# Chunk inverses folded into the operands that read the state, and attention blocks kept within their logits' PSUM banks

## The chip, the core and the metric

The kernel runs on one core of one Trainium2 chip. The metric is the device time of one execution in microseconds, the median over several runs. The engines named below are TensorE (PE, with its weight loads as PEld), VectorE (DVE), ScalarE (ACT), GpSimd (POOL) and SyncE (SP). The PSUM memory that receives matmul results is used here in banks of 128x512 words of 32 bits.

## The reference

One residual block over 512 tokens of 1024 channels, in 32-bit floats:

```
x = x + 0.5 * swiglu(rms_norm(x), w1, w3, w2)            # FFN 1
p = rms_norm(x) @ w_in                                   # r,k,v,codes | q,k,v,f | gates A,B
y_a = rwkv7_mixer(token_shift(p_rwkv)) @ rwkv_proj       # 8 heads x 64
y_b = forgetting_attention(p_fox) @ fox_proj             # 8 heads x 64
x = x + (sigmoid(gA) * y_a + sigmoid(gB) * y_b) @ w_out
x = x + 0.5 * swiglu(rms_norm(x), ...)                   # FFN 2
out = rms_norm(x)

def step(state, inp):                                    # inside rwkv7_mixer, over the 512 tokens
    sa = einsum('bhvk,bhk->bhv', state, a_t)
    state = state * w_t + sa (x) b_t + v_t (x) k_t
    y_t = einsum('bhvk,bhk->bhv', state, r_t)
```

The attention is causal softmax attention whose logits carry a bias, the sum of log forget gates between key and query; q and k are normalized per head.

## The kernel before

**Tiling.** Activations are held transposed, channels on the 128 partitions, 512 tokens in the free dimension. A product of a 1024-row input with 128 columns of a weight matrix is eight `mm3` groups. `mm3` (L122) is three matmuls of 128x128 on 128x512: the weights and the activations are each split in a rounded high part and a remainder, and high x high (L123), high x low (L124) and low x high (L125) are summed. The weights come from DRAM (SP's queue) as `raw`, ACT rounds them to `whi` (L115), DVE subtracts to `wlo` (L116). FFN 1 comes first, then the mixers, the projection `w_out`, FFN 2 and the final norm.

**The recurrence.** The 512 tokens are cut into NC = 16 chunks of C = 32. The eight heads are four pairs p with two halves q. `step(p)` (L507) makes for each pair the operand `G[p][q]` with an a-part (index 0) and an r-part (index 1), and `BK`; products `gp` of BK with G (L569), masked, fill the other 64 rows of G. For the a-part this is the strictly lower triangular matrix L of the chunk, 32x32; it goes to DRAM (`Ld`) and its rows in G are set to zero. After all four steps DVE computes the inverses (I - L)^-1 of all 128 triangles at once (`TT`, L612 and L614, last instruction `inv`), and these go through DRAM (`Td`) into `Tall`, 64-row blocks with two heads each on their diagonal. The loop over chunks (L718) then is, with R the state and the chunk's rows of v and u stacked:

- `xps` = G's a-part on R: eight matmuls (L725), then DVE copies it to `Xs` (L728): first hop
- `ups` = inverse on Xs: four matmuls (L732), then ACT copies it in four pieces into R (L734, L735): second hop
- `sps` = `Dt` on R, the next state: eight matmuls (L739), then two DVE multiplications by the decay PC write it into the next R (L741): third hop
- `yps` = the output, from G's r-part on R (L748), copied by ACT into V4

Every second chunk `stage(c)` (L701) transposes v and BK for two chunks ahead (`vp`, `bp`), and ACT copies them (L713, L714).

**What stands between the hops.** The loop is unrolled, and the scheduler orders the instructions of the whole kernel by its own simulation. Two devices steer it: `tc.issue_after(x)` puts what is inside behind instruction x, and the list `holes` holds matmuls of the chain (two entries each for xps, ups and sps of every chunk) behind which, one after another, the `mm3` groups of columns made by `cols(..., holes)` are put. This filler are the columns of q and k (`load_qk(p)`, L644, bank `pq`) and of gates (`gate`, bank `pgt`, of which `early(m)`, L638, stores the second half's). `plain_gate` (L496) makes a gate's column without holes: eight of these, one inside each step and four ahead of the chunk loop, and eight `early` ones.

**Attention** runs for pairs of heads p = 0..3 beside the chain. For each pair the operands `qa`, `kb`, `klc`, `qb` are made (L786 to L792) on DVE and ACT. Then come three blocks of queries, (0, 1), (2) and (3), each for both halves q: logits `lp` in a bank of `pf` (L804 to L806), maximum on DVE (L812), exponential on ACT (L813), scaling on DVE (L818), transposes (`tpp`, L824) into another bank of `pf`, ACT copy `tr` (L826), the product with v (`av`, L835) in the bank of the second tpp, DVE copy (L837). Pool `pf` has three banks, `pr` (for xps, ups, sps, yps, vp and bp) three, `pm` (for pq and pgt) two. After the loop come the group norm of the recurrence's output (`yc`, `pg`), the two projections and w_out.

Of the kernel before, what the change touches and what calls it, by code (L numbers as in the profile page):

```python
# [9 lines left out]
F32 = mybir.dt.float32  # L10
# [8 lines left out]
P = 128  # L19
T = 512  # L20
# [30 lines left out]
def kernel(  # L51
# [330 lines left out]
    with ExitStack() as mx:  # L382
# [4 lines left out]
        G = [[sp.tile([P, NC, 2, C], F32, name=f"G{p}{q}", tag=f"G{p}{q}") for q in range(2)] for p in range(NP)]  # L387
# [59 lines left out]
        zslots = [h for g in G[3] for h in (g[:, 0:8], g[:, 8:16])] + [BKs[3][:, 0:8], BKs[3][:, 8:16]]  # L447
        zslots = [h.rearrange("p c a t -> p (c a t)") for h in zslots] + spare[0:2]
# [58 lines left out]
        def step(p):  # L507
# [41 lines left out]
            for q in range(2):  # L549
                s = slice(q * 64, (q + 1) * 64)  # L550
                dve.scalar_tensor_tensor(G[p][q][s, :, 0, :], ch(kk)[s], -1.0, Pp[s, :, 0:C],
                                         op0=ALU.mult, op1=ALU.mult)
            for q in range(2):
                s = slice(q * 64, (q + 1) * 64)
                dve.tensor_tensor(G[p][q][s, :, 1, :], ch(r)[s], Pp[s, :, 1:C + 1], op=ALU.mult)
# [4 lines left out]
            gps = [pr.tile([P, 8, 2, C], F32, tag="b", name="gp") for _ in range(2)]  # L560
            for a_ in range(2):
                with tc.issue_after(mms[5].ins):
                    for c in range(8):
                        for q in range(2):
# [4 lines left out]
                            gm = pe.matmul(gps[g][o, c], BK[s, cc], G[p][q][s, cc], start=True, stop=True)  # L569
                for q in range(2):  # L570
# [3 lines left out]
                        G[p][q][o, g * 8:(g + 1) * 8].rearrange("p c a t -> p c (a t)"),  # L574
                        gps[g][o].rearrange("p c a t -> p c (a t)"),
                        gmask[o].rearrange("p a t -> p (a t)").unsqueeze(1).broadcast_to([64, 8, 2 * C]),
                        op=ALU.mult)
            for q in range(2):
                r0 = (1 - q) * 64
                un = (q * NP + p) * NC  # L580
                nc.gpsimd.dma_start(Ld[un:un + NC].rearrange("c s t -> s c t"), G[p][q][r0:r0 + C, :, 0, :])
                pool.memset(G[p][q][r0:r0 + C, :, 0, :], 0.0)
# [33 lines left out]
        Tb = Tall[:].rearrange("p (a c t) -> p a c t", a=2, c=NC)  # L616
        tv = Td[:].rearrange("(q i u) s t -> q i s u t", q=2, i=2)
        for i in range(2):
            for q in range(2):
                o = i * 64 + q * C  # L620
                (nc.scalar, nc.gpsimd)[q].dma_start(
                    Tb[o:o + C].rearrange("p a c t -> p (a c) t")[:, :, q * C:(q + 1) * C], tv[q, i])
# [15 lines left out]
        def early(m):  # L638
            g = xp.tile([P, T], F32, tag="acc", name="gs", bufs=2)
            gate(COL_GB, m, g[:])  # L640
            nc.sync.dma_start(gsave[KD + m], g[:])
# [364 lines left out]
```

## Time and profile before

| | |
|---|---|
| median of 3 runs | 1218.38 us (1218.21 to 1218.86) |
| profiled execution, its own time | 1219.17 us |
| its span in the profile | 1217.5 us |
| mean granted TensorE clock | 0.993 |
| PE, PEld busy share | 98%, 78% |
| DVE, ACT, POOL busy share | 54%, 37%, 8% |

The span goes from the first to the last instruction of the profiled execution. All times are microseconds unless marked ns. L123 is line 123 of the kernel file, and the lines of the changed kernel after the chunk loop stand some 30 lower. In a row of a timeline stand the start, the duration, engine, line, operation, result and operands, shapes, the number of instructions joined in the row and, in brackets, the engine's idle time before it and what ended it. In a row of groups (one that begins with L) stand the busy time of all and the mean ns of one behind the bar, then the engine's idle time ahead of them. In a row of windows stand the length, then busy time and instructions of PE, PEld, DVE, ACT and POOL, the granted clock, the DMA share and the GB/s.

### The profile page before, as it was taken

What the parts mean: (1) busy time and instruction counts of PE and PEld (TensorE: products, weight loads), DVE (VectorE), ACT (ScalarE), POOL (GpSimd) and SP (SyncE); (2) the same over time, 40 slices, a digit from 0 to 9 for tenths busy, and PEclk for the clock granted to TensorE, in tenths of its full rate; (3) what the DMA queues carried; (4) which work ended last, traced back from release to release, by engine and by line L of the source; (5) the groups of instructions that cost most, each with busy time, mean ns of one, the idle gap of its engine ahead of it and who ended that gap; (6) DMA issues with size and microseconds to landing.
All of it is one profiled execution on the core that took longest, in us unless ns stands there. A gap on an engine that the chain in (4) does not pass through costs nothing. (4 is left out here: it accounts for less than half of the span.)

```text
span 1217.5 us, 15845 instructions
## 1 busy us (share of the span) xinstructions
PE 1189.2 (98%) x6340; PEld 954.3 (78%) x6340; DVE 655.5 (54%) x974; ACT 448.9 (37%) x723; POOL 102.5 (8%) x145
## 2 busy tenths in 40 slices
PE   8999999999999999999999998999999999999997
PEld 6888888888887787886766765878888888888887
DVE  6455544543334688686566656665545455442232
ACT  6222222222224754246777547232322222222221
POOL 4100000001111112401000110111000000000110
PEclk9999999999999999999999999999999999999999
DMA  6333333233333333444121250632333333323331
GB/s 185 98 90 101 92 99 104 88 94 113 113 105 100 102 109 105 125 116 110 54 59 62 95 164 26 199 104 87 104 99 91 104 94 97 100 82 95 95 96 69
DMA packets 208088, 122.54 MB, mean 101 GB/s; under 512 B 9902, under 2 KB 200430, under 8 KB 208014
## 3 DMA queue, kind: packets, MB, share of 16 engines
q1 hardware_dynamic: 201934, 108.41, 30.5%
q0 software_dynamic: 3840, 12.32, 3.2%
q10 hardware_dynamic: 2240, 0.79, 0.3%
q8 instruction: 50, 0.82, 0.3%
q14 instruction: 24, 0.20, 0.0%
HBM read 110.82 MB, written 10.68 MB: 100 GB/s over the span
## 5 line engine op out<-in xcount | busy, mean ns | idle before, releaser
L115 ACT CAST whi<-raw 128x1024 fp32r<-128x1024 f32 (+3 forms) x199 | 198.3, 998 | 627.7 <-PE pa L124 178.8
L116 DVE TENSOR_TENSOR wlo<-raw,whi 128x1024 fp32r<-128x1024 f32 (+2 forms) x198 | 229.3, 1159 | 123.7 <-ACT whi L115 121.6
L123 PE MATMUL pa<-xh,whi 128*128 128x512 f32 x344 | 134.6, 391 | 0.0
L125 PE MATMUL pb<-xh,wlo 128*128 128x512 f32 x344 | 133.9, 389 | 0.7 <-DVE wlo L116 0.7
L123 PE MATMUL pb<-xh,whi 128*128 128x512 f32 x344 | 134.2, 390 | 0.0
L125 PE MATMUL pa<-xh,wlo 128*128 128x512 f32 x344 | 133.9, 389 | 0.0
L124 PE MATMUL pa<-xl,whi 128*128 128x512 f32 x344 | 133.8, 389 | 0.0
L124 PE MATMUL pb<-xl,whi 128*128 128x512 f32 x344 | 133.8, 389 | 0.0
L125 PE MATMUL pd<-hh,wlo 128*128 128x512 f32 x330 | 131.2, 398 | 0.0
L123 PE MATMUL pd<-hh,whi 128*128 128x512 f32 x330 | 130.3, 395 | 0.0
L124 PE MATMUL pd<-hl,whi 128*128 128x512 f32 x330 | 130.3, 395 | 0.0
L333 DVE TENSOR_TENSOR fb<-pb,rstd 128x512 f32<-128x512 f32 x43 | 29.7, 691 | 137.2 <-PE pb L125 137.2
L125 PEld LDWEIGHTS pb<-xh,wlo 128*128 128x128 f32 x344 | 64.6, 188 | 14.7 <-DVE wlo L116 1.1
L123 PEld LDWEIGHTS pa<-xh,whi 128*128 128x128 f32 x344 | 64.6, 188 | 13.9 <-issue 0.5
L123 PEld LDWEIGHTS pb<-xh,whi 128*128 128x128 f32 x344 | 64.6, 188 | 13.6 <-ACT whi L115 0.2
L124 PEld LDWEIGHTS pa<-xl,whi 128*128 128x128 f32 x344 | 64.6, 188 | 13.5 <-issue 0.2
L124 PEld LDWEIGHTS pb<-xl,whi 128*128 128x128 f32 x344 | 64.6, 188 | 13.5 <-issue 0.2
L125 PEld LDWEIGHTS pa<-xh,wlo 128*128 128x128 f32 x344 | 64.5, 188 | 13.5
L124 PEld LDWEIGHTS pd<-hl,whi 128*128 128x128 f32 x330 | 62.0, 188 | 14.9
L123 PEld LDWEIGHTS pd<-hh,whi 128*128 128x128 f32 x330 | 62.0, 188 | 14.8 <-issue 0.2
L125 PEld LDWEIGHTS pd<-hh,wlo 128*128 128x128 f32 x330 | 62.0, 188 | 14.8 <-issue 0.2
L329 DVE TENSOR_TENSOR fa<-pa,rstd 128x512 f32<-128x512 f32 x43 | 29.7, 692 | 73.1 <-PE pa L125 72.9
(367 smaller groups left out, 1960.8 us busy)
## 6 DMA issues: line engine op xcount, KB each, us to landing
raw<-in_ffn_w_dram SPq DMA_DIRECT2D x118, 512.0 KB
raw<-in_w_in_dram SPq DMA_DIRECT2D x40, 512.0 KB
raw<-in_ffn_w_dram SPq DMA_DIRECT2D x15, 384.0 KB
raw<-in_w_out_dram SPq DMA_DIRECT2D x8, 512.0 KB
xin<-in_x_dram SPq DMA_DIRECT2D x4, 512.0 KB
xsave<-xT POOLq DMA_DIRECT2D x8, 256.0 KB, 2.3
gsave<-gs POOLq DMA_DIRECT2D x8, 256.0 KB, 2.6
gsave<-gs SPq DMA_DIRECT2D x8, 256.0 KB
```

Of the source, the lines that this page charges most:

```text
L115: act.copy(hi[:], raw[:])
L116: (eng or dve).tensor_tensor(lo[:], raw[:], hi[:].bitcast(F32), op=ALU.subtract)
L123: pe.matmul(ps, whi, xhi, start=first, stop=False)
L124: pe.matmul(ps, whi, xlo, start=False, stop=False)
L125: return pe.matmul(ps, wlo, xhi, start=False, stop=last)
L329: dve.tensor_tensor(a[:], pa[:], nrm.rstd[:], op=ALU.mult)
L333: dve.tensor_tensor(b[:], pb[:], nrm.rstd[:], op=ALU.mult)
```

## The change

**The inverses.** The operand that reads the state is multiplied by the inverse once, ahead of the loop, so that `ups` comes from R in one step. `G` is laid out as [2][NC][C] instead of [NC][2][C], so that the a-part of four chunks is one contiguous 128-column block. After the columns of v, PE transposes these blocks (32 transposes, `gtr`) and ACT copies them to `GT`. `Tall` is now filled as `Tn`, with the inverses of two neighbouring chunks of one head on the diagonal of a 64x64 block. 64 matmuls `wps` multiply GT by Tn, and 16 evictions, half on ACT and half on DVE, write the result over G's a-part. In the loop, xps, Xs and the old ups are gone; eight matmuls `ups` read G and R, and one ACT copy and one DVE copy put the result in R.

**Filler.** `holes` gets two entries each for ups and sps of a chunk, and five for wps. `load_qk` is split in `load_qk` (columns) and `norm_qk`. The columns of pair 1 are made ahead of the recurrence, and the gate column NP + 3 moves from there into `early`: seven plain gates and nine early ones. The decay logs and the norm of pair 1 are put behind the first chunk's state eviction (`begun`) instead of behind `inv`.

**Attention.** The transposes go into the bank of their own logits, and `av` into the second of these; a block uses two banks of pf.

```diff
-        G = [[sp.tile([P, NC, 2, C], F32, name=f"G{p}{q}", tag=f"G{p}{q}") for q in range(2)] for p in range(NP)]
+        G = [[sp.tile([P, 2, NC, C], F32, name=f"G{p}{q}", tag=f"G{p}{q}") for q in range(2)] for p in range(NP)]
...
-        Tb = Tall[:].rearrange("p (a c t) -> p a c t", a=2, c=NC)
-        tv = Td[:].rearrange("(q i u) s t -> q i s u t", q=2, i=2)
...
+        Tn = Tall[:].rearrange("p (u t) -> p u t", t=2 * C)
+        tv = Td[:].rearrange("(u g i) s t -> g i s u t", g=2, i=2)
+        for g in range(2):
+            for i in range(2):
+                o = g * 64 + i * C
+                (nc.scalar, nc.gpsimd)[i].dma_start(Tn[o:o + C, :, i * C:(i + 1) * C], tv[g, i])
...
-        def early(m):
+        def early(n):
+            m = n + NP + 3
             g = xp.tile([P, T], F32, tag="acc", name="gs", bufs=2)
-            gate(COL_GB, m, g[:])
-            nc.sync.dma_start(gsave[KD + m], g[:])
+            gate(COL_GA, m, g[:])
+            nc.sync.dma_start(gsave[m], g[:])
...
-        def load_qk(p):
+        def load_qk(p, holes=()):
             both = []
             for c0, par0 in ((COL_Q, PAR_Q), (COL_KF, PAR_K)):
...
+                mix.cols(ps[:], *load_w(win(c0 + p * P), KD, P), P, holes)
+                if p < NP // 2:
+                    act.copy(o[:], ps[:])
+                else:
+                    dve.tensor_tensor(o[:], ps[:], mix.rstd[:], op=ALU.mult)
...
+        def norm_qk(p):
+            if p < NP // 2:
+                for o, par0 in qks[p]:
+                    dve.tensor_tensor(o[:], o[:], mix.rstd[:], op=ALU.mult)
...
+        for q, p in [(q, p) for q in range(2) for p in range(NP)]:
+            ps = bank("gtr", pr)
+            for j in range(4):
+                pe.transpose(ps[:, j * P:(j + 1) * P], G[p][q][:, 0, j * 4:(j + 1) * 4, :].rearrange("p c t -> p (c t)"), ident[:])
+            GT[q, p] = t2.tile([P, T], F32, name=f"GT{p}{q}", tag=tags[q * NP + p])
+            act.copy(GT[q, p][:], ps[:])
         plain_gate(NP)
         plain_gate(NP + 1)
         load_qk(0)
-        plain_gate(NP + 2)
-        ahead = plain_gate(NP + 3)[-1]
+        load_qk(1)
+        ahead = plain_gate(NP + 2)
+        with tc.issue_after(inv.ins):
+            norm_qk(0)
...
+        for q in range(2):
+            for p0 in range(0, NP, 2):
+                wps = [pr.tile([P, 2, 4, 2 * C], F32, tag="b", name="wps") for _ in range(2)]
+                with tc.issue_after(ahead[2 * q + p0 // 2 + 4].ins):
+                    for p in (p0, p0 + 1):
+                        for j in range(4):
+                            for g in range(2):
+                                hw = pe.matmul(wps[g][:, p - p0, j, :], GT[q, p][half(g), j * P:(j + 1) * P],
+                                               Tn[half(g), (q * NP + p) * 4 + j, :], start=True, stop=True)
+                for p in (p0, p0 + 1):
+                    for g in range(2):
+                        to = G[p][q][:, 0].rearrange("p (j g i) t -> p g j (i t)", g=2, i=2)[:, g]
+                        if g:
+                            act.copy(to, wps[g][:, p - p0])
+                        else:
+                            dve.tensor_copy(to, wps[g][:, p - p0])
+                holes.append(hw)
+        holes.append(hw)
...
-            xps = pr.tile([P, 2, 64], F32, tag="b", name="xps")
+            ups = pr.tile([P, NP, 64], F32, tag="b", name="ups")
             for p, q in heads():
...
-            Xs = sp.tile([P, 2, 64], F32, tag="Xs", name="Xs", bufs=2)
-            dve.tensor_copy(Xs[:], xps[:])
-            ups = pr.tile([P, 2, 64], F32, tag="b", name="ups")
-            for p in range(NP):
-                h = half(p // 2)
-                hu = pe.matmul(ups[h, p % 2, :], Tb[h, p % 2, c, :], Xs[h, p % 2, :], start=True, stop=True)
-            for i in range(2):
-                act.copy(R[64:96, 2 * i:2 * i + 2, 0, :], ups[64 * i:64 * i + 32])
-                act.copy(R[0:32, 2 * i:2 * i + 2, 1, :], ups[64 * i + 32:64 * i + 64])
+                o = (1 - q) * 64
+                hu = pe.matmul(ups[o:o + C, p, :], G[p][q][:, 0, c, :], R[:, p, q, :], start=True, stop=True,
+                               tile_position=(0, o))
+            act.copy(R[64:96, :, 0, :], ups[64:96])
+            dve.tensor_copy(R[0:32, :, 1, :], ups[0:32])
...
-            holes += [hx, hx, hu, hu, hs, hs]
+            holes += [hu, hu, hs, hs]
+            if c == 0:
+                begun = decay
...
-        aside.enter_context(tc.issue_after(inv.ins))
+        aside.enter_context(tc.issue_after(begun.ins))
...
+        norm_qk(1)
         aside.close()
-        load_qk(1)
...
-                    tpp = pf.tile([P, T], F32, tag="b", name="tpp")
-                    tpps.append(tpp)
+                    tpp = lps[q]
...
-                av = tpps[1]
+                av = lps[1]
...
-                if p < NP // 2 and i == 0:
-                    load_qk(p + NP // 2)
-                elif p == 1 and i == 2:
-                    early(0)
-                    early(1)
-                elif p >= NP // 2:
-                    early(3 * p - 4 + i)
+                if p == 0 and i < 2:
+                    load_qk(i + 2, holes)
+                    norm_qk(i + 2)
+                elif 3 * p + i < 3 * NP - 1:
+                    early(3 * p - 2 + i)
```

The rest of the diff adapts the other readers of G to its new layout, and applies the last gate columns' tanh only where `gate` has not done it.

**What moves.** PE ahead of the loop. Before, the last columns of the gate (pgt) are followed directly by the first chunk's xps:

```order
L124 MATMUL pgt<-xl_2596,whi 128x512
L125 MATMUL pgt<-xh_2595,wlo 128x512
L123 MATMUL pgt<-xh_2689,whi 128x512
L124 MATMUL pgt<-xl_2690,whi 128x512
L125 MATMUL pgt<-xh_2689,wlo 128x512
L725 MATMUL xps<-RD_4196,G_2702 32x64
L725 MATMUL xps<-RD_4196,G_2703 32x64
```

Now the products wps stand there, in two stretches among filler, and the first ups follows the last of them (the numbers tell buffers apart; GT_3999 to GT_4020 are the four pairs of the second half q):

```order
L743 MATMUL wps<-Tall,GT_3999 128x64 x8
L743 MATMUL wps<-Tall,GT_4006 128x64 x8
L743 MATMUL wps<-Tall,GT_4013 128x64 x4
L743 MATMUL wps<-Tall,GT_4020 128x64 x4
L123 MATMUL pq<-xh_2125,whi 128x512
L124 MATMUL pq<-xl_2126,whi 128x512
L125 MATMUL pq<-xh_2125,wlo 128x512
L123 MATMUL pq<-xh_2219,whi 128x512
L124 MATMUL pq<-xl_2220,whi 128x512
L743 MATMUL wps<-Tall,GT_4013 128x64 x4
L743 MATMUL wps<-Tall,GT_4020 128x64 x4
L763 MATMUL ups<-RD_4284,G_2702 32x64
L763 MATMUL ups<-RD_4284,G_2703 32x64
```

Where columns of a gate stood ahead of the chain, wps and columns of q stand.

DVE at the same place in the changed kernel: copies of wps into G (L751), operands of the first pair of attention heads (L820 to L823), and then the first chunk's copy of ups into R (L766). The names are those of the section on the kernel:

```order
L820 TENSOR_TENSOR qa_5085<-qk_4090,qa_5085 64x512
L751 COPY G_2706<-wps 128x4x64
L751 COPY G_2708<-wps 128x4x64
L821 CAST kb_5086<-qk_4123 64x512
L822 CAST kb_5086<-qk_4123 64x512
L823 TENSOR_TENSOR klc_5045<-qk_4123,kb_5086 64x512
L821 CAST kb_5087<-qk_4123 64x512
L822 CAST kb_5087<-qk_4123 64x512
L823 TENSOR_TENSOR klc_5046<-qk_4123,kb_5087 64x512
L751 COPY G_2703<-wps 128x4x64
L751 COPY G_2705<-wps 128x4x64
L751 COPY G_2707<-wps 128x4x64
```

The evictions of the second half's wps stand behind four casts and two differences.

DVE at the change from one pair of heads to the next, before; the row of L741 is the state's eviction:

```order
L788 CAST kb_5654<-qk_5218 64x512
L789 CAST kb_5654<-qk_5218 64x512
L792 CAST qb_5114<-sel 64x512
L812 TENSOR_REDUCE mx_5367<-lp 128x1
L790 TENSOR_TENSOR klc_5013<-qk_5218,kb_5654 64x512
L788 CAST kb_5655<-qk_5218 64x512
L789 CAST kb_5655<-qk_5218 64x512
L792 CAST qb_5115<-sel 64x512
L812 TENSOR_REDUCE mx_5368<-lp 128x1
L787 TENSOR_TENSOR qa_5652<-qk_5183,qa_5652 64x512
L741 TENSOR_TENSOR RD_4196<-sps,PC 64x4x64 x2
```

And now; L772 is the state's eviction, L766 the copy of ups:

```order
L772 TENSOR_TENSOR RD_4284<-sps,PC 64x4x64 x2
L820 TENSOR_TENSOR qa_5438<-qk_4156,qa_5438 64x512
L821 CAST kb_5441<-qk_4189 64x512
L822 CAST kb_5441<-qk_4189 64x512
L825 CAST qb_5083<-sel 64x512
L845 TENSOR_REDUCE mx_5103<-lp 128x1
L848 RECIPROCAL mx_5102<-mx_5102 128x1
L820 TENSOR_TENSOR qa_5439<-qk_4156,qa_5439 64x512
L673 SCALAR_TENSOR_TENSOR qk_5307<-qk_5307,par,qrn 128x512
L823 TENSOR_TENSOR klc_5046<-qk_4189,kb_5441 64x512
L766 COPY RD_4284<-ups 32x4x64
```

The operands that stood ahead of a state's eviction now stand between one and the copy of ups.

65 lines of the change are left out of this document (27 added, 38 removed).

## The prediction

> **What bounds the kernel now.** I read the page first: is there an engine that could give time back by being relieved?
>
> ```profile
> span 1217.5 us, 15845 instructions
> PE 1189.2 (98%) x6340; PEld 954.3 (78%) x6340; DVE 655.5 (54%) x974; ACT 448.9 (37%) x723; POOL 102.5 (8%) x145
> ```
>
> TensorE (PE) is at work for 1189.2 of 1217.5 us. The change can therefore win in two ways only: by taking matmul work away, or by closing the 28 us in which PE waits, together with what a reduced clock costs. So the second view is the busy time by stretches of 20 us through the stage that the change touches (PE, PEld, DVE, ACT, POOL, then the granted clock):
>
> ```profile
> 541.00:561.00 20.00, 18.87 (x100) 14.47 (x98) 12.70 (x29) 9.55 (x18) 3.83 (x8) 1.00 0.73 185
> 561.00:581.00 20.00, 18.86 (x197) 13.85 (x196) 16.19 (x28) 15.29 (x35) 0.00 (x0) 1.00 0.10 28
> 581.00:601.00 20.00, 20.00 (x225) 15.77 (x222) 9.80 (x24) 14.47 (x41) 0.00 (x0) 1.00 0.19 54
> 661.00:681.00 20.00, 18.15 (x185) 13.46 (x181) 12.71 (x28) 12.85 (x34) 0.55 (x1) 0.91 0.20 61
> 721.00:741.00 20.00, 15.56 (x85) 9.84 (x84) 6.73 (x17) 10.76 (x22) 1.64 (x3) 0.83 0.36 120
> 741.00:761.00 20.00, 18.10 (x65) 11.77 (x65) 16.99 (x28) 16.09 (x28) 0.00 (x0) 1.00 0.09 27
> 541.00:701.00 160.00, 151.67 (x1468) 113.75 (x1467) 100.91 (x215) 108.16 (x266) 8.21 (x16) 0.99 0.28 80
> ```
>
> From 541 to 701 us, nearly the whole recurrence, PE waits for 160 - 151.67 = 8.3 us, and the clock of 0.91 in one stretch costs 0.09 x 20 = 1.8 us more. The end of attention, 721 to 761 us, waits 4.44 + 1.90 = 6.3 us and loses 0.17 x 20 = 3.4 us of clock. That is 19.8 us, all that there is to win besides work. Third, which waits these are, from PE's timeline:
>
> ```profile
> 557.30 0.49 PE L140 MATMUL pq<-shi,bonesr 128*128 128x512 f32 x1 [0.58 <-ACT shi L136]
> 558.76 0.44 PE L732 MATMUL ups<-Xs,Tall 64*64 64x64 f32 x4 [0.47 <-DMA Tall<-Td]
> 570.03 0.33 PE L739 MATMUL sps<-RD,RD 128*64 128x64 f32 x2 [1.09 <-ACT RD L734]
> 626.87 0.30 PE L725 MATMUL xps<-RD,G 128*32 128x64 f32 x2 [1.70 <-DVE RD L741]
> 630.23 0.46 PE L732 MATMUL ups<-Xs,Tall 64*64 64x64 f32 x8 [0.86 <-DVE Xs L728]
> 658.81 0.45 PE L725 MATMUL xps<-RD,G 128*32 128x64 f32 x16 [0.93 <-ACT RD L713]
> 669.36 0.30 PE L725 MATMUL xps<-RD,G 128*32 128x64 f32 x2 [1.69 <-DVE RD L741]
> 728.85 1.55 PE L835 MATMUL tpp<-tr,vt 128*64 128x128 f32 x12 [2.98 <-ACT tr L826]
> ```
>
> The reader is to see that the hop which is removed (xps, its copy Xs, then ups) owns little of it: 0.86 us stands at Xs in these rows. The largest two wait for the state's eviction on VectorE (DVE, L741), a hop that stays. Why DVE is late there is in its own timeline:
>
> ```profile
> 664.32 0.42 DVE L792 CAST qb<-sel 64x512 fp32r<-64x512 f32 x1
> 664.77 0.69 DVE L812 TENSOR_REDUCE mx<-lp 128x1 f32<-128x512 f32 x1
> 665.50 0.68 DVE L790 TENSOR_TENSOR klc<-qk,kb 64x512 fp32r<-64x512 f32 x1
> 666.21 0.42 DVE L788 CAST kb<-qk 64x512 fp32r<-64x512 f32 x1
> ...
> 668.17 0.69 DVE L787 TENSOR_TENSOR qa<-qk,qa 64x512 fp32r<-64x512 f32 x1
> 668.89 0.88 DVE L741 TENSOR_TENSOR RD<-sps,PC 64x256 f32<-64x256 f32 x2
> ```
>
> At the change from one pair of attention heads to the next, the operands of the new pair (qa, kb, qb, klc) stand ahead of the state's eviction in DVE's queue, and PE, out of filler, waits at 669.36. So the waits come from the load on DVE and ScalarE (ACT) at certain places, not from the number of hops.
>
> **The change part by part.** PE's filler (the columns of gates, q and k) is the same in number before and after and cancels. What differs:
>
> *Removed: the ups hop*, 16 bursts of 4 matmuls. What one costs is the distance of the filler around it:
>
> ```profile
> 566.57 0.39 PE L125 MATMUL pq<-xh,wlo 128*128 128x512 f32 x1
> 566.89 0.46 PE L732 MATMUL ups<-Xs,Tall 64*64 64x64 f32 x8
> 567.28 0.50 PE L123 MATMUL pq<-xh,whi 128*128 128x512 f32 x1
> ...
> 568.54 0.40 PE L125 MATMUL pq<-xh,wlo 128*128 128x512 f32 x1
> ```
>
> From 566.57 to 567.28 is 0.71 us, where fillers follow each other at 0.23: 0.48 us a burst, 16 x 0.48 = 7.7 us. The new ups burst has the shape of the old xps burst and costs the same.
>
> *Added: 32 transposes of G and 64 products wps.* Nothing is idle to hide them: PE is full from 521 to 554. For prices there are these rows:
>
> ```profile
> 677.15 1.04 PE L824 MATMUL tpp<-ident,pts 128*128 128x128 f32 x8
> 677.94 0.31 PE L804 MATMUL lp<-kb,qa 128*128 128x128 f32 x1
> L569 PE MATMUL gp<-G,BK 64*64 64x64 f32 x256 | 9.4, 221 | 0.0
> L713 ACT COPY RD<-vp 32x256 f32<-32x256 f32 x32 | 11.6, 362 | 3.3 <-PE vp L704 2.9
> L741 DVE TENSOR_TENSOR RD<-sps,PC 64x256 f32<-64x256 f32 x30 | 12.6, 421 | 8.3 <-PE sps L739 7.9
> ```
>
> Eight transposes take (677.94 - 677.15) = 0.79 us to the next matmul, 0.10 to 0.11 each: 32 give 3.5 us. wps is not in the trace. Its nearest row is gp: also two passes a matmul, also alternating between the halves of the rows, but 64 columns of stationary operand where wps has 128: 9.4 / 128 = 73 ns a matmul. If the columns cost nothing, 64 x 0.073 = 4.7 us; if a pass costs what a transposed 128-column block costs, 128 x 0.11 = 14 us; doubled with the columns, 9.4 us, in which the ends of gp's bursts are counted too. I take 8. Work: 3.5 + 8 - 7.7 = +3.8 us, between +0.5 and +10.
>
> The Trainium skill (TensorE: Matmul & The Clock Gate, LDWEIGHTS) speaks against a cheap wps: a load costs by its columns, whatever its rows, 128 / 1.2 = 107 ns. By it alone 128 loads are 13.7 us and the sum below is 5.7 us higher; its page TensorEngine Tiling (Array Packing), Key Properties, lets the two 64-row tiles load in parallel, which halves that. No run here shows wps.
>
> *New wait: getting wps out.* A pair of heads needs two of the three banks, and 16 evictions of 128x256, about 0.42 us by the L741 row, are split between ACT and DVE. In the new order DVE's eviction of q = 0 comes behind qa, and that of q = 1 behind six operand casts and differences (kb, kb, klc twice: 4 x 0.42 + 2 x 0.69 = 3.1 us). PE's matmuls follow in order, so everything behind them waits too. Walking through it: pair 2 waits 1.2 us for a bank (qa cast, qa, two evictions), pair 3 0.6, pair 4 1.9 behind the six, the first ups 0.7 for the last evictions: 4.4 us. Against it goes the wait for the inverses' DMA, 0.58 + 0.47 = 1.05 us before (the rows at 557.30 and 558.76), since PE now comes some 10 us later. Net +3.3; 0 if DVE is through with the casts earlier, 5 if not.
>
> *The chain itself.* Two hops, each still covered by two groups of three fillers: 567.28 to 568.54 and 0.23 more, 1.5 us. A third of the hops goes, and four ACT copies of a hop become one and one on DVE. But filler leaves the chain too: 187 matmuls stand between its first and last ups where 300 stood, 113 x 0.227 = 26 us, and all of ACT's and DVE's work for norms and attention there stays. With the 16 chunks of 2 hops, PE has about 107 us of work there (151 us from first to last xps, less 26, less 7.7, less 9 of waits and clock, less 2 of attention that falls later). Summing the instructions between the first and the last ups in the new order at the durations of their groups, ACT has 86 us and DVE 86: 0.80 of the time, where the window row has 108.16 / 160 = 0.68 and 100.91 / 160 = 0.63. One place as an example, chunk 8 of the new order, the change to the second pair of heads: between the state's eviction and the copy of ups stand qa, kb, kb, qb, a maximum, a reciprocal, qa, a norm's product, klc: 0.69 + 0.42 + 0.42 + 0.42 + 0.69 + 0.16 + 0.69 + 0.75 + 0.69 = 4.9 us, then the copy, 0.4. PE has against that the ups burst (0.46), two groups (1.5) and two logit blocks (0.7): it waits 2.7 us. On ACT the fourth chunk has 10.3 us of work against 7.7 of PE. So I expect 9 us of waits and 2 us of clock in the chain where 7.3 and 1.8 stand now: +2. From below, if the present waits shrink with the hops to two thirds or vanish: -3 to -9; from above, if every heavy place waits like chunk 8: +10.
>
> The Trainium skill (TensorE: Matmul & The Clock Gate, Why this matters for your kernels) would count no clock here, since it asks only that gaps stay under about 3 us. The row at 661 us has 0.91 with no gap above 1.7 us, so the rows decide; by the page the sum is 2 us lower.
>
> *Attention in its logits' banks.* No instruction is saved; transposes and products write to other banks. Two banks a block instead of four of three let the next logits start earlier. In the chain filler covers that already. At the end the wait of 2.98 us is ACT's (a copy behind a gate's tanh and a table load), which stays; the last logits may come a step sooner: -1 (0 to -4).
>
> Sum: 3.8 + 3.3 + 2 - 1 = **+8 us** on the profiled execution, which took 1219.17 us (span 1217.5). The three runs shown have a median of 1218.38, so the forecast is 1218.4 + 8 = **1226.5 us**.
>
> **Rivals.** *The waits go with the hops.* One mechanism, in chunks 0 to 15: one late engine less for each chunk, evictions on two engines side by side, and the casts never outlast the filler. Then the 7.3 us and 1.8 us of clock vanish instead of growing by 2: 3.8 + 3.3 - 9.1 - 1 = -3, with wps at 7.4 (128 passes at 58 ns, gp's pace doubled without its ends) -3.6: 1214.8 us, faster. It decides once the chain's waits stay under some 3 us in all. For it: 581 to 601 us, four chunks' worth of hops, without any wait. Against it: the waits sit where DVE is full, and DVE gets fuller. *Half of that* gives 3.8 + 3.3 - 5 - 1 = +1: no change, about 1219.4. *The heavy side:* wps serial at 0.11 us a pass (+6), and two more stretches at half clock, about 1.7 us each (the 1.8 at 661): 8 + 6 + 3.4 = +17.4, 1236 us. For it speak the clock row and that the waits come bunched.
>
> **How the numbers follow.** Forecast 0.50 (its own range 1221 to 1232), faster 0.24, no change 0.12, heavy side 0.14. From the three bounds together the range is 1212 to 1240: below lie only the cases in which setup waits vanish as well, above all upper ends at once. 0.2% (2.4 us) is about what a measurement of this kernel can tell from no change. Faster 0.24, same 0.12, slower 0.64.
>
> **What would show it.** In the new profile: wps busy about 8 us in two bursts near 565 us, transposes of G 3.5 us; PE waits at wps or the first ups, released by DVE, of 3 to 5 us; waits at ups and sps released by DVE RD and ACT RD of about 9 us, the longest where kb and klc of the second and third pair stand; ACT and DVE at 0.8 in the chain; the end of attention nearly as before. The forecast is wrong if the chain shows less than 3 us of waits, if wps costs under 5 us, or if the end of attention loses its 2.98 us wait and its half clock.

## The result, and the profile after

The changed kernel takes 1230.32 us (median of 6 runs, 1227.55 to 1230.90) against 1218.62 us for the kernel before in the same comparison (6 runs, 1218.14 to 1221.97): ratio 1.0088, 95% interval 1.0074 to 1.0103. It is slower by 11.7 us. The profiled execution took 1229.89 us. The first lines of its page, answering to those of before:

```profile
span 1228.2 us, 15898 instructions
PE 1206.2 (98%) x6372; PEld 975.1 (79%) x6372; DVE 661.5 (54%) x982; ACT 445.6 (36%) x692; POOL 100.5 (8%) x144
```

PE works 17.0 us longer in a span that is 10.7 us longer, so it waits 6.3 us less: 22.0 us against 28.3. The change did shorten the waits. The view by stretches of 20 us (PE, PEld, DVE, ACT, POOL, granted clock) shows what took more than that; the last row answers to the one of before below it:

```profile
541.00:561.00 20.00, 20.00 (x93) 16.41 (x92) 12.47 (x27) 11.94 (x21) 2.71 (x6) 1.00 0.60 150
561.00:581.00 20.00, 19.95 (x141) 17.71 (x139) 10.41 (x20) 9.16 (x18) 0.57 (x1) 0.75 0.26 69
581.00:601.00 20.00, 19.22 (x156) 15.06 (x155) 9.37 (x15) 8.17 (x19) 0.00 (x0) 0.82 0.10 27
641.00:661.00 20.00, 17.96 (x160) 13.66 (x159) 16.51 (x34) 16.21 (x36) 0.00 (x0) 0.91 0.10 27
721.00:741.00 20.00, 20.00 (x109) 15.94 (x108) 13.46 (x31) 8.84 (x21) 1.64 (x3) 1.00 0.37 115
541.00:781.00 240.00, 232.01 (x1824) 180.12 (x1823) 150.04 (x306) 142.87 (x312) 12.11 (x23) 0.96 0.29 82
```

```profile
541.00:781.00 240.00, 225.33 (x1843) 167.57 (x1842) 149.06 (x307) 148.98 (x347) 17.46 (x33) 0.98 0.31 92
```

Between 541 and 781 us PE waits 8.0 us instead of 14.7. But the clock is 0.75 and 0.82 from 561 to 601 us, which costs 0.25 x 20 + 0.18 x 20 = 8.6 us, in two stretches where PE is busy 19.95 and 19.22 of 20 us. What runs there is in PE's timeline (rows of filler left out):

```profile
565.50 3.78 PE L743 MATMUL wps<-Tall,GT 64*128 64x64 f32 x48
...
570.22 8.87 PE L743 MATMUL wps<-Tall,GT 64*128 64x64 f32 x64
579.01 0.79 PE L123 MATMUL pq<-xh,whi 128*128 128x512 f32 x1
...
581.45 3.67 PE L743 MATMUL wps<-Tall,GT 64*128 64x64 f32 x16
585.05 1.07 PE L763 MATMUL ups<-RD,G 128*32 128x64 f32 x16
```

The products wps hold PE without a gap (a matmul of them is two passes), and the granted clock falls to one half at 571.2 us and stays there to 588.2, as short windows show around the fall:

```profile
569.00:571.00 2.00, 1.95 (x13) 1.41 (x13) 1.72 (x5) 1.95 (x5) 0.00 (x0) 1.00 0.87 250
571.00:573.00 2.00, 2.00 (x17) 2.00 (x17) 1.94 (x5) 0.42 (x1) 0.00 (x0) 0.54 0.00 0
```

The first 48 passes take 3.71 us (77 ns each), the last 16 take 3.60 us (225 ns each). By the start times in the trace the first 32 come in pairs, one on each half of the rows, 56 ns a pass; the next 24, up to the fall of the clock, come singly, 112 ns each.

The longest wait rows that are left in the chain, and those of the end of attention:

```profile
614.07 0.33 PE L770 MATMUL sps<-RD,RD 128*64 128x64 f32 x2 [1.16 <-ACT RD L765]
652.75 0.84 PE L724 MATMUL bp<-ident,BK 128*128 128x128 f32 x4 [1.57 <-ACT RD L730]
743.90 0.88 PE L866 MATMUL lp<-tr,vt 128*64 128x128 f32 x12 [0.45 <-ACT tr L857]
748.73 0.63 PE L855 MATMUL lp<-ident,pts 128*128 128x128 f32 x4 [0.61 <-ACT pts L846]
```

The waits of 1.70 and 1.69 us at DVE's state eviction are gone, and so is the 2.98 us at the end of attention with its half clock.

For all runs the same account can be made from the trace: the time from each matmul's start to the next one's, with PE's waits taken out and what a halved clock adds taken out ("work"), then the waits, then what the clock added. Against the profiled execution of the kernel named, in us (1.7 us of clock are the program's start, where the first half clock lasts 6.83 us instead of 3.41 in the profiled executions of the change, the inverse alone and two banks: they stand with a plus in these three rows, and with a minus in the three rows against the change):

| run | against | span | work | waits | clock |
|---|---|---|---|---|---|
| the change | before | +10.7 | +10.3 | -6.2 | +6.8 |
| banks alone | before | -13.1 | -0.9 | -7.6 | -4.5 |
| inverse alone | before | +16.5 | +10.4 | -2.2 | +8.5 |
| paired, dense | the change | -8.2 | -1.2 | +1.5 | -8.5 |
| paired, spread | the change | -16.7 | -1.6 | -5.4 | -9.6 |
| four groups | the change | +10.4 | +3.3 | +3.2 | +3.9 |
| spread, four groups | paired, spread | +15.7 | +3.5 | +5.6 | +6.5 |
| two banks | banks alone | +17.2 | +0.3 | +5.8 | +11.1 |

### The profile page after: what moved, and what is told of

The parts are those of the page before. It is cut to its first block, busy times and chain, and to the rows that moved or that the text cites. A ratio compares the mean times of both kernels' runs of the same rounds, so it can differ in the third digit from the quotient of the medians.

```text
span 1228.2 us, 15898 instructions
## 1 busy us (share of the span) xinstructions
PE 1206.2 (98%) x6372; PEld 975.1 (79%) x6372; DVE 661.5 (54%) x982; ACT 445.6 (36%) x692; POOL 100.5 (8%) x144
```

## The experiments

### The two halves of the change apart

The attention part alone, put into the kernel before:

```diff
-                tpps = []
                 for q in range(2):
-                    tpp = pf.tile([P, T], F32, tag="b", name="tpp")
-                    tpps.append(tpp)
+                    tpp = lps[q]
...
-                av = tpps[1]
+                av = lps[1]
```

> The kernel before, with only the attention blocks moved into their logits' banks. In the changed kernel PE's waits after the last ups fell from 6.3 to 2.1 us and the half clock there (3.4 us) went. Theory: that came from filler, of which 117 matmuls instead of 49 are left behind the last ups; then the banks alone leave the 2.98 us wait and the half clock at the end, and the time is that of before, 1217 to 1220 us. Rival: the banks gave it (the next logits start earlier), then 5 to 8 us go: 1211 to 1214 us and no half clock near 729 us.

Measured: 1207.15 us (1206.21 to 1209.10), before 1219.67; ratio 0.9899, interval 0.9883 to 0.9915. The rival holds, and by more than it said: the banks alone win 12.5 us with the filler where it was. It is the fastest kernel of this study. The last logits of attention, before and in this kernel, on PE's timeline:

```profile
733.16 0.78 PE L804 MATMUL lp<-kb,qa 128*128 128x512 f32 x1
...
739.81 1.09 PE L835 MATMUL tpp<-tr,vt 128*64 128x128 f32 x16
```

```profile
714.82 0.40 PE L804 MATMUL lp<-kb,qa 128*128 128x512 f32 x1
726.76 1.09 PE L833 MATMUL lp<-tr,vt 128*64 128x128 f32 x16
```

The chain's last ups runs at 709 us in both, but attention's last logits come 18.3 us earlier. When the chain ends, 31 of the 32 logit blocks are done instead of 24 (counted at L804). So little attention is left for the stretch in which no chain covers it, and the windows show the same: PE busy for 19.61 us at full clock where it was 15.56 at 0.83, and a chain whose clock holds.

```profile
541.00:701.00 160.00, 154.57 (x1529) 119.27 (x1528) 110.54 (x244) 114.42 (x286) 8.21 (x16) 1.00 0.29 78
721.00:741.00 20.00, 19.61 (x77) 11.68 (x77) 14.09 (x24) 15.30 (x25) 1.10 (x2) 1.00 0.38 116
```

DVE and ACT are busier in the chain than before (110.54 and 114.42 us against 100.91 and 108.16), and PE still waits 2.9 us less there.

The other half, the changed kernel with the bank part undone:

```diff
-                    tpp = lps[q]
+                    tpp = pf.tile([P, T], F32, tag="b", name="tpp")
+                    tpps.append(tpp)
...
-                av = lps[1]
+                av = tpps[1]
```

> The changed kernel with tpp and av back in banks of their own. Theory: the banks give nothing that filler does not give, so 1229 to 1232 us, with the long half clock near 571 us unchanged. Rival: the banks are worth the end of attention, then 1235 to 1238 us. A third way: with tpp in banks of its own pf runs short and the chain waits more, 1232 to 1235 us.

Measured: 1235.97 us (1235.63 to 1239.04), before 1219.67; ratio 1.0139, interval 1.0121 to 1.0156. The rival holds: the banks are worth 5.7 us in the changed kernel. The two halves do not add: -12.5 and +16.3 make +3.8, the change is +11.7. With the inverse part in it the chain begins 31 us later (ups at 585.05, xps at 554) and the first logits 15 us later (601 against 586 us), and when the chain ends 22 of the 32 blocks are done. What the banks win alone is that attention runs further ahead in the chain, and that the inverse part takes back: in the changed kernel it is 22 blocks with the banks and without. There their gain is 4.0 us of waits and 1.7 us of clock, half of the waits within the chain. The longest wait of the chain with the inverse alone, for DVE's eviction of the state (L772) behind operands of the next heads, is not in the changed kernel:

```profile
683.55 1.52 PE L763 MATMUL ups<-RD,G 128*32 128x64 f32 x16 [2.20 <-DVE RD L772]
```

Why the banks remove it was not tried.

Two banks instead of three for the kernel with the banks alone:

```diff
-    pf = ctx.enter_context(tc.tile_pool(name="pf", bufs=3, space=PSUM))
+    pf = ctx.enter_context(tc.tile_pool(name="pf", bufs=2, space=PSUM))
```

> The kernel with the attention banks alone (1207.2 us), with two banks in that pool instead of three. Theory: what the bank change gave is the free third bank, into which the next block's logits go while this one is transposed and multiplied; with two banks blocks run one behind the other and most of the gain is lost: 1214 to 1222 us. Rival: the gain comes from the shorter way within a block, not from the third bank: 1206 to 1209 us.

Measured: 1223.53 us (1223.34 to 1224.11), before 1218.48; ratio 1.0042, interval 1.0027 to 1.0057. The theory holds, and the loss is above its upper end: without the third bank all of the gain is gone and 5 us more. It is lost where the chain no longer covers attention:

```profile
721.00:741.00 20.00, 14.04 (x67) 8.38 (x64) 7.13 (x20) 6.94 (x19) 0.55 (x1) 0.60 0.05 15
```

PE waits 5.96 us there and the clock is 0.60. The longest of the waits:

```profile
725.17 1.51 PE L822 MATMUL lp<-ident,pts 128*128 128x128 f32 x6 [2.10 <-DVE mx L815]
```

A block's transposes wait for its own softmax, and by the code the next block's logits have no bank. The pool also holds the sums for the norms of q and k (`pq2`), which now share the two banks; what that costs was not separated.

### The price of wps and the clock

wps with its two banks from two pools, so that the halves of the rows alternate throughout:

```diff
-                wps = [pr.tile([P, 2, 4, 2 * C], F32, tag="b", name="wps") for _ in range(2)]
+                wps = [o_.tile([P, 2, 4, 2 * C], F32, tag="b", name="wps") for o_ in (pr, pf)]
```

> The changed kernel with wps' second bank taken from pf, so that the two 64-row halves alternate in all 128 passes; still one unbroken stretch, where the changed kernel has half the passes on one half only (112 ns each against 56 ns). Theory: a long stretch of wps itself lowers the clock, whatever its order. 128 x 0.056 = 7.2 us at full clock instead of 10.4, but the half clock comes all the same and lasts two to five windows of 3.41 us (3.4 to 8.5 us lost): 1223 to 1229 us. Rival: the clock fell because the unpaired loads leave the array half empty; then no half clock near 571 us and 3.2 + 8.5 us are saved: 1217 to 1220 us.

Measured: 1222.05 us (1220.85 to 1222.88), before 1219.67; ratio 1.0018, interval 1.0009 to 1.0028. The time is the theory's, the mechanism the rival's, as PE's timeline shows:

```profile
563.91 7.36 PE L743 MATMUL wps<-Tall,GT 64*128 64x64 f32 x128
572.35 0.27 PE L763 MATMUL ups<-RD,G 128*32 128x64 f32 x2 [1.08 <-DVE G L751]
574.34 0.76 PE L763 MATMUL ups<-RD,G 128*32 128x64 f32 x8 [1.72 <-DVE G L751]
```

All 128 passes run in 7.36 us, 57.5 ns each, at full clock. The half clock comes at 573.1 us, after the wait of 1.08 us and in that of 1.72, and lasts 6.83 us. DVE's timeline shows what they wait for:

```profile
571.46 0.74 DVE L751 COPY G<-wps 128x256 f32<-128x256 f32 x2
572.23 0.42 DVE L821 CAST kb<-qk 64x512 fp32r<-64x512 f32 x1
...
573.14 0.69 DVE L823 TENSOR_TENSOR klc<-qk,kb 64x512 fp32r<-64x512 f32 x1
573.86 1.42 DVE L751 COPY G<-wps 128x256 f32<-128x256 f32 x4
```

The evictions stand behind the casts and differences of the first heads, as the prediction had it (0.6 to 1.9 us a wait). In the changed kernel no such wait appears, because there wps itself takes so long.

The same order with two groups of filler after every 16 passes (diff cut; the columns of q and k of pair 2 are taken from the chain for it):

```diff
+        last = ahead[-1]
         for q in range(2):
             for p0 in range(0, NP, 2):
-                wps = [pr.tile([P, 2, 4, 2 * C], F32, tag="b", name="wps") for _ in range(2)]
-                with tc.issue_after(ahead[2 * q + p0 // 2 + 4].ins):
-                    for p in (p0, p0 + 1):
+                wps = [o_.tile([P, 2, 4, 2 * C], F32, tag="b", name="wps") for o_ in (pr, pf)]
+                for p in (p0, p0 + 1):
+                    with tc.issue_after(last.ins):
...
+                    with tc.issue_after(hw.ins):
+                        for k in range(2 * p, 2 * p + 2):
+                            last = mm3(pqs[q][:], wq[q][0][:, k, :], wq[q][1][:, k, :],
+                                       mix.hi[k][:], mix.lo[k][:], k == 0, k == KD - 1)
```

> As the paired order, but the eight blocks of 16 passes are separated by two groups of three filler matmuls each (the columns of q and k of pair 2, which are made here instead of in the chain). Theory: between filler the clock holds, no half clock from 565 to 600 us; wps costs 7.2 us and about 2 us of entries and exits of the eight bursts, against 10.4: 8.5 + 1 us less than the changed kernel, 1219 to 1222 us, if the chain does not miss the filler taken. Rival: the small matmuls lower the clock even spread, or the half clock has another cause (the inverse's end, the evictions): 1226 to 1231 us. Second rival: the chain misses the filler and its waits of 5.8 us rise above 9: 1223 to 1226 us with the clock full near 571 us.

Measured: 1213.13 us (1212.94 to 1213.22), before 1219.67; ratio 0.9945, interval 0.9929 to 0.9962. That is 17.2 us less than the changed kernel and 6 us below the expected range.

```profile
564.07 1.11 PE L748 MATMUL wps<-Tall,GT 64*128 64x64 f32 x16
565.11 0.50 PE L123 MATMUL pq<-xh,whi 128*128 128x512 f32 x1
...
566.69 1.11 PE L748 MATMUL wps<-Tall,GT 64*128 64x64 f32 x16
...
561.00:581.00 20.00, 20.00 (x163) 15.47 (x162) 10.75 (x19) 9.46 (x17) 0.57 (x1) 1.00 0.35 92
```

The clock holds, as the theory said, and the evictions and casts are hidden. What it had not said is the 5.4 us of waits: in the chain PE waits 3.3 us instead of 5.8 and after it 1.4 instead of 3.0, though the chain gave filler away; 28 of the 32 logit blocks are done when it ends, against 22. Why attention gets ahead there was not tried by itself.

What makes the clock fall? Three kernels put 64 matmuls of wps' shape, whose results nothing reads, into the kernel before. The first stands ahead of the chain, in the changed kernel's order (diff cut):

```diff
+        for q in range(2):
+            for ps_ in (((0, 1), (0, 1)), ((2, 3), (0,)), ((2, 3), (1,))):
...
+                                ahead = pe.matmul(wps[i][:, p % 2, j, :], vs[p][half(g), j * P:(j + 1) * P],
+                                                  Tall[half(g), u * 64 % 1024:u * 64 % 1024 + 64], start=True, stop=True)
```

> The kernel before with 64 matmuls of the shape of wps ahead of the first chunk, in the changed kernel's order (a quarter of them paired, a quarter on one half of the rows, and so twice), whose results nothing reads: no evictions, no GT, the rest as before. Theory: the stretch by itself takes 10.4 us at full clock and lowers the clock after about 5 us, as at 571 us in the changed kernel; 3.4 to 8.5 us lost more, and up to 2 us of waiting for the inverses, which are now needed earlier: 1232 to 1240 us, with a half clock that begins inside the stretch and no idle time of PE before it. Rival: the clock fell for another reason (evictions, what follows on PE); then it holds here and the time is 1229 to 1231 us.

Measured: 1244.20 us (1242.33 to 1246.21), before 1218.48; ratio 1.0211, interval 1.0194 to 1.0227. It does not settle the cause of the fall, since PE waited 5.67 us for the inverses just ahead and the clock fell in that wait. It shows the other direction:

```profile
562.00 20.16 PE L697 MATMUL wps<-Tall,V 64*128 64x64 f32 x128 [5.67 <-DMA Tall<-Td]
```

For 20 us PE has no gap, and the clock stays at one half to the end of the stretch (27.3 us in all).

The second and third stand between two columns of a gate, where PE is full on both sides and nothing has to be waited for. In one the halves alternate, in the other 32 passes run on one half and then 32 on the other, twice:

```diff
-        plain_gate(NP)
-        plain_gate(NP + 1)
+        ahead = plain_gate(NP)[-1]
+        for _ in range(2):
+            wps = [pr.tile([P, 16, C], F32, tag="b", name="wps") for _ in range(2)]
+            with tc.issue_after(ahead.ins):
+                for j, g in [(j, g) for j in range(16) for g in range(2)]:
...
+        with tc.issue_after(ahead.ins):
+            plain_gate(NP + 1)
```

> The kernel before with 64 matmuls of the shape of wps between two columns of a gate, where PE is full on both sides; they read rows of V, nothing reads their results. Here the two 64-row halves alternate. In the paired, dense kernel the clock held through 7.4 us of wps and fell only after two waits; so theory: the clock holds, and 128 x 0.056 = 7.2 us and an entry and exit of 0.2 us are added: 1225 to 1227 us. Rival, the theory up to now: a dense stretch of these lowers the clock in any order: 3.4 us of half clock or more, 1229 us or above.

> The same 64 matmuls at the same place, in the other order: 32 passes on one half of the rows and then 32 on the other, twice. Theory: a pass takes 0.112 us at full clock, as in the changed kernel, and a stretch on one half lowers the clock within two windows of 3.41 us and holds it down until it ends: 14.3 us of work and 5 to 10 us of clock, 1237 to 1244 us, with no wait of PE ahead of the fall. Rival: the order costs only the loads, then 14.3 us and no half clock: 1232 to 1234 us.

Measured: 1232.63 us (1230.91 to 1233.44) and 1243.01 us (1236.88 to 1244.46), before 1218.85; ratios 1.0112 (1.0095 to 1.0128) and 1.0185 (1.0155 to 1.0214). The second is as the theory said: the clock falls at 529.1 us, 3.1 us into the stretch, with PE full, and stays down for 23.9 us.

```profile
526.00 22.39 PE L689 MATMUL wps<-V 64*128 64x64 f32 x128
...
521.00:541.00 20.00, 20.00 (x114) 18.87 (x113) 17.88 (x42) 2.82 (x4) 0.56 (x1) 0.70 0.24 66
541.00:561.00 20.00, 20.00 (x85) 17.53 (x85) 3.74 (x11) 1.53 (x2) 3.28 (x7) 0.70 0.32 78
```

One of its four runs took only 1236.88 us, at a mean clock of 0.989 where the others have 0.982 to 0.984; it has no trace, so how long its half clock lasted is not known.

The first missed, for its order was not the one that was written: the scheduler, short of a bank, had taken the second half's passes apart, as in the changed kernel. So it was made again with one pair of banks for all:

```diff
+        wps = [pr.tile([P, 16, C], F32, tag="b", name="wps") for _ in range(2)]
+        for _ in range(2):
```

> As the paired dead stretch, now with one pair of banks for all 64 matmuls, so that the halves alternate through all 128 passes (in the run before, the scheduler took half of them apart: 62 passes came in pairs until 529.25 us with the clock full, and it fell at 531.78, after 2.5 us of single passes). Theory: paired passes hold the clock, single ones do not: 7.2 us of work and no half clock near 530 us, 1225 to 1227 us. Rival: a dense stretch of these lowers the clock in any order; then it falls by 532 us again and the time is 1228 to 1233 us.

Measured: 1233.03 us (1230.68 to 1235.49), before 1219.60; ratio 1.0117, interval 1.0090 to 1.0144. The clock did what the theory said, the time did not. PE's stretch and its window:

```profile
524.99 7.36 PE L689 MATMUL wps<-V 64*128 64x64 f32 x128
...
521.00:541.00 20.00, 20.00 (x184) 17.48 (x184) 18.09 (x44) 1.81 (x3) 0.56 (x1) 1.00 0.25 67
```

The same number of passes at the same place, 7.36 us, at full clock throughout in this execution, whose mean clock is 0.993; the other three runs have 0.989 to 0.991, and where they lost it no trace shows (the kernel before has 0.989 to 0.995 in the same comparison). The time was spent later:

```profile
548.25 0.69 PE L123 MATMUL pq<-xh,whi 128*128 128x512 f32 x1 [4.57 <-ACT gs L503]
...
546.66 1.04 ACT L115 CAST whi<-raw 128x1024 fp32r<-128x1024 f32 x1 [20.26 <-issue]
```

PE waits 4.57 us for a copy of a gate's column (second row: ACT's timeline). ACT stands idle for 20 us before that, since its queue holds the inverses' transfers, issued only when DVE has them, ahead of its next cast. That the scheduler had reckoned with a PE that gets there later is an inference. 6.8 us of work and 4.3 us of waits make the profiled difference of 11.4 with 0.4 of clock.

### The price of the new ups

```diff
-            ups = pr.tile([P, NP, 64], F32, tag="b", name="ups")
+            ups = pr.tile([P, 2, 64], F32, tag="b", name="ups")
...
-                o = (1 - q) * 64
-                hu = pe.matmul(ups[o:o + C, p, :], G[p][q][:, 0, c, :], R[:, p, q, :], start=True, stop=True,
+                o = (p // 2) * 64 + q * C
+                hu = pe.matmul(ups[o:o + C, p % 2, :], G[p][q][:, 0, c, :], R[:, p, q, :], start=True, stop=True,
...
-            act.copy(R[64:96, :, 0, :], ups[64:96])
-            dve.tensor_copy(R[0:32, :, 1, :], ups[0:32])
+            for i in range(2):
+                act.copy(R[64:96, 2 * i:2 * i + 2, 0, :], ups[64 * i:64 * i + 32])
+                dve.tensor_copy(R[0:32, 2 * i:2 * i + 2, 1, :], ups[64 * i + 32:64 * i + 64])
```

> The changed kernel with the eight matmuls of ups written to four groups of 32 rows (as xps was) instead of two, and moved into R by two copies each on ACT and DVE. Theory: the prediction's price for the new ups was wrong because its passes share two groups of columns of the array: start to start at full clock ups takes 9.9 us in all, the old xps 6.9. On four groups it falls back to about 6.9: 3 us less, 1226 to 1228.5 us; the extra copies are short and covered. Rival: the price comes from something else (the operands, the neighbours), then 1229.5 to 1231 us, or more by the extra copies.

Measured: 1242.58 us (1240.35 to 1244.49), before 1218.48; ratio 1.0196, interval 1.0179 to 1.0214. The price is explained and the time is not. One burst of 16 passes in the changed kernel, and here:

```profile
594.23 0.64 PE L763 MATMUL ups<-RD,G 128*32 128x64 f32 x16
```

```profile
611.59 0.44 PE L763 MATMUL ups<-RD,G 128*32 128x64 f32 x16
```

ups falls from 9.9 to 6.7 us in all, as xps had it. But two copies more on each engine and chunk are not covered. The chain's waits rise from 5.8 to 11.2 us, among them these:

```profile
681.90 0.33 PE L771 MATMUL sps<-RD,RD 128*64 128x64 f32 x2 [1.29 <-ACT RD L766]
685.31 0.58 PE L771 MATMUL sps<-RD,RD 128*64 128x64 f32 x5 [1.07 <-DVE RD L767]
```

and sps, yps and attention's matmuls take 6.1 us of work more, nearly twice what ups saves. Why these cost more was not tried; they stand in more and shorter bursts.

The same edit on the paired and spread kernel:

> The paired and spread kernel with ups on four groups too: the inverse part at its best as far as the traces show. Theory: the two savings add, 1213.1 - 3 = 1209 to 1211.5 us, so that it ends above the kernel with the banks alone (1207.2): its work is still some 6 us more than there (transposes 3.2 and wps 8.3, against about 6 for the hop) and its waits are 4 us less. Rival: a hop less pays when its operands are cheap, then below 1206 us.

Measured: 1227.54 us (1226.02 to 1228.91), before 1218.48; ratio 1.0070, interval 1.0052 to 1.0087. Neither holds; it is 14.4 us slower than without the edit. ups falls from 9.5 to 6.0 us, the waits rise by 5.6 and the clock takes 6.5 more. In both kernels DVE and ACT do 8 to 12 us more in the chain than without the edit. When the chain ends, 28 and 32 of the 32 logit blocks are done, against 22 and 28 without it: attention that runs ahead does not by itself make a kernel faster, here the chain takes 17 and 20 us longer.

## Why the prediction was right, and where it was not

The direction, the time (1226.5 us forecast, 1230.32 measured) and the range are right. The reason given for most of it is not: two large terms were missed with opposite signs, and that they nearly cancel is luck. For the inverse part the terms add up to +9.1 us (3.8 + 3.3 + 2), and alone it costs 16.3; for the banks the term is -1, and in the changed kernel they win 5.7. All work together came to +10.3 us, just above the prediction's upper end of +10.

**What bounds the kernel: right.** PE is full, and only work, waits and clock can change. All three did.

**The ups hop, -7.7 us forecast: mis-sized.** The two old bursts took 6.9 + 6.5 us, the new one takes 9.9; with 2.0 us less for the rest of PE's work, above all the filler that they interrupted, and 2.2 us more for yps, about 3.3 us were saved. The step that failed is "The new ups burst has the shape of the old xps burst and costs the same": it has the same operands, but writes two groups of 32 rows where xps wrote four, and 16 passes take 0.64 us instead of 0.45. The four groups bring that back (0.44).

**The transposes of G, 3.5 us: right.** They took 3.2.

**wps, 8 us between 4.7 and 14: the mechanism was right and the size a little low, its main cost was not foreseen.** At full clock it took 10.4 us. Two of the prediction's prices are both there, gp's pace doubled without its ends (58 ns) and a transposed block's 0.11 us, since about half of the passes alternate (57.5 ns in the paired kernel's 128) and the rest do not (the last 16 take 225 ns each at half clock, so 112). The lowest bound, columns that cost nothing, is not. The Trainium skill (TensorE: Matmul & The Clock Gate, LDWEIGHTS) lets a load take its columns divided by 1.2, in ns, an estimate of 107 ns for 128 columns; the 112 ns agree. The Trainium skill (TensorEngine Tiling (Array Packing), Key Properties) lets different tiles load in parallel; the 57.5 ns, about half of that, agree. But no term stood for a clock that falls while PE is busy: 8.6 us by the windows of the changed kernel. That it is the passes on one half that do it is shown by the pair of dead stretches: alternating, 7.36 us at full clock; one half after the other, the clock falls after 3.1 us. Whether it falls because half of the rows stand idle, or because each pass waits for its load of weights, is not shown, since the two go together in these runs. The Trainium skill (TensorE: Matmul & The Clock Gate, Why this matters for your kernels) asks only that PE has no idle gaps above about 3 us; here PE had none, and the measurement decides. In the prediction the clock was bound to waits as well.

**Setup waits, +3.3 us: wrong in the changed kernel, -1.0.** The wait for the inverses' DMA went as said. The waits for evictions did not come, because the scheduler ran the passes on one half of the rows while the other bank was being emptied, which is what made them slow. In the paired, dense kernel, where it could not, waits of 1.08 and 1.72 us for DVE stand at the first ups.

**Chain waits and clock, +2 us: about right for the inverse part, taken back by the banks.** In the changed kernel the chain's waits fell from 7.3 to 5.8 us (the 8.3 of the window before hold the 1.05 of setup), and its clock went from 1.7 to 3.3 us, of which 1.6 is the end of wps' half clock. In the kernel with the inverse alone they are 7.9 us of waits and, without the end of wps' half clock, 3.4 of clock: +2.3 together. Its wait of 2.20 us is of the kind that the prediction reads from DVE's timeline before, at another change of heads than its example of 2.7 us (chunk 8): qb, a maximum and qa stand ahead of the state's eviction. So it was not the hop less that shortened the waits, as the rival has it, and they did not come under its 3 us either; the banks did. ACT and DVE were busy for 0.66 of the chain (80.0 of 120.35 us each), not 0.8, since the chain took longer than 107 us and held less of their work than 86. That load on ACT and DVE makes waits fits the kernels with four groups: they add copies and no hop, and lose 12.3 and 14.4 us, of which 3.2 and 5.6 are waits.

**Attention in its logits' banks, -1 us between 0 and -4: wrong by an order of magnitude.** Alone it is -12.5 us, in the changed kernel -5.7. The step that failed is "In the chain filler covers that already. At the end the wait of 2.98 us is ACT's (a copy behind a gate's tanh and a table load), which stays": the wait went; in the kernel with the banks alone this is because with a free bank attention runs ahead and most of its end moves under the chain. Nor did filler cover the chain already: the banks took 2.9 us of waits and 1.7 of clock out of it in the kernel before, and 2.0 and 1.7 in the changed one. The releaser named in a row tells who came last, not what had made the whole block late. The prediction had named the loss of this wait as what would refute it.

So the change is the sum of a large gain and a larger loss, and the forecast of +8 hit +11.7 because it left out one of each.

## What to carry to other kernels

Measure the parts of a change apart before the sum is believed: here one half, two lines, makes the kernel 1.0% faster, and the other half hides it. Even paired and spread, and with the banks beside it, the inverse part leaves the kernel 6 us slower (1213.13 us) than the banks alone (1207.15). Small matmuls on 64 rows are to alternate between the halves of the array and to be spread among full ones, and the order that the scheduler makes of them is to be read, since a missing bank is enough to take the pairs apart. Where a dependent chain is covered by other work, PSUM banks that let that work run ahead can be worth more than a hop less in the chain.

## What the chip showed that was not expected

- The granted clock falls to one half, and stays there, while PE has no gap at all: with 64-row passes mostly on one half of the array at a time for 22 us (clock 0.70 over 521 to 561 us with PE busy 40.00 of 40 us). Passes that alternate held full clock for 7.36 us, but one stretch of 20.16 us that began at half clock, with part of its passes alternating, was not released.
- 16 passes of 32 columns take 0.44 us when they write four groups of rows and 0.64 us when they write two.
- All half clocks in these traces but the one at each program's end last 3.41 us or a multiple of it (6.83, 10.24, 17.07, 20.48, 23.89, 27.31 us), so that one wait of 1 to 2 us can cost 1.7 us of clock on top: before, the clock fell 1.2 us after the wait of 1.69 us at 669.36 us had ended, for 3.41 us.
